# Hybrid attention and retention trunk on one core: a TensorE order written out at build time for the attention stage, the first query and key projection moved ahead of the last retention block, and part of the output projection run as filler

## The chip, the cores and the metric

The kernel runs on one core of one Trainium2 chip. The core has TensorE (PE in the profile, its weight loads apart as PEld), VectorE (DVE), ScalarE (ACT), GpSimd (POOL) and SyncE (SP), which issues most of the DMAs. The metric is the device time of one execution in microseconds, median of several runs.

## The reference, cut to what matters

Two layers, each the same; 1024 tokens, width 1024, everything in float32:

```python
def hybrid_layer(x, ...):
    proj = x @ w_in                      # fox q|k|v|forget logits, ret q|k|v|gate
    fox_out = fox_attention(q, k, v, log_sigmoid(f + b))   # 8 heads of 64, causal softmax,
                                         # logits = q k / 8 + c_i - c_j, c = cumsum(log_f)
    ret = groupnorm(retention_chunkwise(rotary(rq), rotary(rk), rv, gamma))   # 4 heads of 128
    mix = concat([fox_out, silu(rg) * ret]) @ w_out
    x = layernorm(ALPHA * x + mix)
    return layernorm(ALPHA * x + square(relu(x @ w_ff1)) @ w_ff2)
```

## The kernel before

Every float32 matrix is split into a rounded part and a rest (`split`, L159: ACT copies the rounded part, DVE subtracts), and a product is three PE matmuls (`mm3`, L229: low by high, high by low, high by high). One `mm3` over one slice of 128 inputs is thus three matmuls of 128x512; it is the unit called a step of filler below.

A layer runs in these stages (`layer`, L653). **Values and forget sums**: `project_values` (L309) and `forget_sums` (L338), which leaves the cumulated biases of all heads in the DRAM tensor c_d. **Retention**: for each of two pairs of heads, r = 0 and 1, `retention` (L370) projects queries and keys (block rqk), then gates and values (block rgv), eight token tiles each; the matmuls of scores and outputs follow two and three tiles later through `defer` and `tick`, and results go to r_d. **Queries and keys**: `project_qk` (L469) projects one pair p of attention heads in 36 steps (32 hold an `mm3`, four hold the evacuation) and writes q_d and k_d in DRAM; pair 0 comes right after the retention. **Attention** (`attention`, L495). **Output projection** in two column halves (L784 to L801). **Feed-forward**, a Strassen form in two parts (`feed_forward_in`, `feed_forward_out`).

Attention works on 32 blocks of steps (h, qq): head h, query rows 256*qq to 256*qq+255. For each it runs

- fronts (F; `front`, L525): for each of two row blocks one or two chunks of scores, two matmuls of queries by keys each (L541), and with the last chunk a mask matmul (L545). DVE adds the bias rel and takes the maximum (L547), ACT does the exponential (L553), DVE the reciprocal (L555), POOL scales (L556). A head has 12 chunks.
- backs (B; `back`, L560): for each pair of key blocks, a turn, 3 or 4 PE transposes of probabilities into one PSUM bank (L569), then a split into pt by ACT (L161) and DVE (L162). A head has 10 turns.
- values (V; `values`, L579): four matmuls per turn of pt by the values vp (L591); after every second block ACT and DVE add two halves (L604, L605), and for odd heads split them into mix.

`load` (L498) fetches queries, keys (ks) and values (vp) of a head from q_d, k_d and v_d, by SP, two buffers each. `load_bias` (L511) fetches one head's row of c_d to all partitions in ncb, one buffer, and `bias` (L518) makes rel from it on POOL, one buffer for each qq.

While attention runs, PE also gets filler, the generator `rest` (L699): `project_qk` of pairs 1 to 3 (108 steps), then `ret_transposes` (L488), eight groups of four PE transposes of retention outputs, each fetched from r_d into one buffer.

The program is written by a merge (L610): for block i the backs of i, the fronts of block i+2 (DEPTH = 2, L48) and a number of filler steps by `FILL` (L50): 18 for each head up to 5, then 4. Values trail the backs by up to 5 turns (LAG). That written order is only a priority: the scheduler of the framework places each instruction when its simulation finds it ready, PE's too, so later matmuls may fill earlier gaps. `load(h+1)` is called in block (h, 0) and `load_bias(h+1)` in block (h, 1), when fronts are at (h, 3); rel of (h, 3) is made by `bias` after the fronts of (h, 2). On SP, as on each engine, instructions then run in the order that the scheduler gave.

The output projection takes chunks of two 128-wide slices of the 1024 mixed inputs; slices 0 to 3 are the attention pairs, 4 to 7 retention. Its first half (L784 to L792) runs chunks in the order 4, 6, 0, 2 over eight token tiles in eight PSUM banks, its weights prepared up to two ahead (`weight`, L224, with a ring of four).

## Time and profile before

| | |
|---|---|
| median of 3 runs | 2405.14 us (2402.55 to 2405.2) |
| the profiled execution | 2406.83 us, of which the span 2404.8 us |
| PE busy | 2361.1 us, 98% of the span |
| DVE, ACT, POOL busy | 63%, 42%, 14% |
| mean granted PE clock | 0.997 of full speed |

Busy is the time in which at least one instruction of an engine is under way. Matmuls overlap: one of 128x512 lasts about 0.39 us, and one follows another in much less, so a short pause between two starts leaves PE busy. What a matmul costs is therefore read from the distance of starts. In the first layer attention runs from 313 to 517 us of the span, in the second from 1503 to 1707.

### The profile page before, as it was taken

The numbers are of one execution on the slowest core, as the hardware profiler recorded it, in microseconds if no ns is written. First come the engines' busy times: TensorE is split into PE (matmuls) and PEld (weight loads), VectorE is DVE, ScalarE is ACT, GpSimd is POOL, SyncE is SP. The second block draws the span as 40 slices with busy tenths as digits, with TensorE's granted clock in tenths as the row PEclk, the third lists the DMA queues.
The fourth block names the chain that finished last, engine by engine and source line by source line (L and its number), as shares of the span: only waits on it lengthen the run. The fifth ranks groups of instructions, "written<-read, shape, count | busy, mean of one in ns | idle before, by whom it ended". The sixth has DMA issues, their size and how long they took to land.

```text
span 2404.8 us, 32463 instructions
## 1 busy us (share of the span) xinstructions
PE 2361.1 (98%) x11888; PEld 1983.0 (82%) x11888; DVE 1510.0 (63%) x2703; ACT 1015.2 (42%) x1556; POOL 337.0 (14%) x469
## 2 busy tenths in 40 slices
PE   8999999999999999999999999999999999999997
PEld 8888887887888888888898888888888888888886
DVE  4655447854876667665755554588467766676557
ACT  3222246735544553434321212477274444543331
POOL 0223223500000000000202322244000000000003
PEclk9999999999999999999999999999999999999999
DMA  7465676433364458667555567664334544586664
GB/s 233 165 220 207 216 212 183 123 119 113 109 221 148 145 188 310 211 210 223 179 164 187 209 212 231 182 177 116 132 101 147 199 164 148 213 294 214 196 194 145
DMA packets 243807, 442.47 MB, mean 184 GB/s; under 512 B 26032, under 2 KB 128432, under 8 KB 235456
## 3 DMA queue, kind: packets, MB, share of 16 engines
q1 hardware_dynamic: 241344, 432.01, 55.2%
q10 hardware_dynamic: 2304, 8.39, 0.9%
q8 instruction: 94, 1.54, 0.3%
q14 instruction: 65, 0.53, 0.1%
HBM read 301.85 MB, written 138.48 MB: 183 GB/s over the span
## 4 chain that ended last, share of the span: by engine, by line
PE 88%; DMA 4%; DVE 4%; ACT 1%; issue 1%; SPq 0%; POOL 0%; DVEq 0%; ACTq 0%; POOLq 0%
PE mm L233 17%; PE qk L233 11%; PE qk L860 9%; PE tr L1070 7%; PE pv L1070 7%; PE pv L860 7%; PE qk L1070 5%; PE mm L1070 5%; PE mm L860 5%; PE tr L860 4%; PE tr L569 2%; PE qk L541 2%; PE pv L591 2%; DMA q_d<-ev 1%; PE pv L233 1%
## 5 line engine op out<-in xcount | busy, mean ns | idle before, releaser
L162 DVE TENSOR_TENSOR elo<-est,ehi 128x1024 fp32r<-128x1024 f32 x216 | 261.2, 1222 | 180.3 <-ACT ehi L161 179.4
L161 ACT CAST ehi<-est 128x1024 fp32r<-128x1024 f32 x216 | 226.7, 1054 | 343.4 <-PE pv L1070 127.5
L233 PE MATMUL mm<-whi,act 128*128 128x512 f32 (+1 forms) x608 | 187.9, 375 | 0.9 <-DVE act L162 0.5
L233 PE MATMUL qk<-whi,act 128*128 128x512 f32 (+1 forms) x608 | 186.6, 373 | 0.8 <-DVE act L162 0.8
L860 PE MATMUL qk<-xop,whi 128*128 128x512 f32 x608 | 187.3, 389 | 0.0
L161 ACT CAST whi<-wst 128x512 fp32r<-128x512 f32 (+1 forms) x140 | 115.9, 830 | 165.8 <-PE qk L233 36.0
L286 POOL TENSOR_SCALAR sd<-mv 128x1 f32<-128x1 f32 x15 | 13.9, 928 | 1211.4 <-DVE mv L283 1211.0
L860 PE MATMUL pv<-xop,whi 128*128 128x512 f32 x512 | 157.7, 389 | 0.0
L162 DVE TENSOR_TENSOR wlo<-wst,whi 128x512 fp32r<-128x512 f32 (+1 forms) x140 | 132.0, 946 | 39.2 <-ACT whi L161 38.6
L860 PEld LDWEIGHTS qk<-xop,whi 128*128 128x128 f32 x608 | 114.2, 188 | 23.6
L162 DVE TENSOR_TENSOR pt<-tr,pt 128x512 fp32r<-128x512 f32 (+1 forms) x160 | 99.7, 631 | 46.5 <-ACT pt L161 45.8
L233 PEld LDWEIGHTS mm<-whi,act 128*128 128x128 f32 x608 | 112.6, 192 | 19.7 <-ACT whi L161 0.8
L591 PE MATMUL pv<-pt,vp 128*128 128x256 f32 (+1 forms) x640 | 127.5, 302 | 0.2
L233 PE MATMUL mm<-act,whi 128*128 128x512 f32 x384 | 125.9, 396 | 0.0
L233 PEld LDWEIGHTS qk<-whi,act 128*128 128x128 f32 x608 | 110.3, 189 | 18.7 <-DVE act L162 1.0
L553 ACT ACTIVATE sc<-sc,mx 128x128 f32<-128x128 f32 (+7 forms) x128 | 99.4, 777 | 51.9 <-DVE mx L547 44.4
L860 PE MATMUL mm<-xop,whi 128*128 128x512 f32 x384 | 118.6, 390 | 1.5 <-DVE xop L162 1.5
L860 PE MATMUL qk<-xop,wlo 128*128 128x512 f32 x304 | 118.6, 390 | 0.0
L556 POOL TENSOR_SCALAR sc<-sc,ri 128x128 f32<-128x128 f32 (+7 forms) x128 | 96.8, 762 | 136.7 <-DVE ri L555 104.8
L161 ACT CAST pt<-tr 128x512 fp32r<-128x512 f32 (+1 forms) x160 | 85.8, 541 | 70.0 <-PE tr L569 67.9
L233 PE MATMUL mm<-wlo,act 128*128 128x512 f32 (+1 forms) x304 | 113.7, 374 | 0.7 <-DVE wlo L162 0.7
L860 PEld LDWEIGHTS pv<-xop,whi 128*128 128x128 f32 x512 | 96.1, 188 | 20.0
(278 smaller groups left out, 5942.8 us busy)
## 6 DMA issues: line engine op xcount, KB each, us to landing
est<-h_d SPq DMA_DIRECT2D x224, 256.0 KB, 3.6
wst<-in_w_ff_dram SPq DMA_DIRECT2D x76, 512.0 KB, 4.3
wr<-in_w_ff_dram SPq DMA_DIRECT2D x32, 1024.0 KB, 5.1
t_d<-ts SPq DMA_DIRECT2D x32, 1024.0 KB, 4.2
h_d<-hs SPq DMA_DIRECT2D x32, 1024.0 KB, 5.5
est<-t_d SPq DMA_DIRECT2D x128, 256.0 KB, 4.0
h_d<-rest SPq DMA_DIRECT2D x32, 768.0 KB, 5.7
est<-in_w_ff_dram SPq DMA_DIRECT2D x96, 256.0 KB, 4.8
```

The lines of the kernel that those rows point to most:

```text
L161: A.copy(hi, src)
L162: V.tensor_tensor(lo, src, hi.bitcast(F32), op=ALU.subtract)
L233: PE.matmul(ps, lhs(a, k), rhs(b, k), start=first and i == 0 and j == 0, stop=last and i == n - 1 and j == 2)
L286: G.tensor_scalar(sd, mv[:, :, 1], EPS, 1.0, op0=ALU.add, op1=ALU.mult)
L541: PE.matmul(ps[:, 0:w], qs[:, rb * P : rb * P + P], ks[part][:, c0 : c0 + w], start=part == 0, stop=part == 1 and not last)
L553: A.activation(sc[:, 0:ne], sc[:, 0:ne], AF.Exp, bias=mx, scale=-1.0, accum_out=sm)
L556: G.tensor_scalar(sc[:, 0:ne], sc[:, 0:ne], ri, 1.0, op0=ALU.mult, op1=ALU.mult)
L569: PE.transpose(tr[:, 2 * i + rb, :], probs[rb][:, j * P : j * P + P], ident)
L591: PE.matmul(ob[:, c + f * P : c + 256], vp[:, js[i], :], pt[b][:, 2 * i + f : 2 * i + 2, :], start=qq % 2 == 0 and jp == 0 and n == 0 and ...
L860: PE.matmul(ps, ops[p][a][:, k, :], right[p][b][:, k, :], start=first and k == 0 and n == 0, stop=last and k == 3 and n == 2, skip_group_c ...
L1070: PE.matmul(ps, ops[x_][:, 0, i * P : i * P + P], ops[y][:, 1, :], start=first and n == 0, stop=last and n == 2, skip_group_check=True)
```

## The change

A function `attention_order` writes the order of all attention work on PE as a list of letters: F one chunk, B one turn's transposes, V one turn's value matmuls, X one step of filler. It walks a model of DVE, ACT and POOL as three queues with durations written into it, and picks what is ready: V before B before F before X, but X first where filler is behind a goal, a line through fixed marks (30 steps before the first chunk, 36 by chunk 16, 72 by 40, 108 by 64, 128 by 96), with at most 4 steps ahead of it. Fronts may be 12 chunks ahead of the backs and three blocks of steps, and pt has three buffers. The letters alone reach the kernel; attention is emitted in their order in a region in which PE keeps the written order (where these instructions fall among PE's instructions from outside the region is left to the scheduler).

```diff
+DEPTH = 12
 QK_STEPS = 36
+WO_FIRST = 4
+RET_STEPS = 8
+WO_STEPS = 12
+SLACK = 4
+FIRST = 30
+LANDING = 9.0
+MARGIN = 1.2
+def attention_order():
...
+    qk_x = QK_STEPS * 3
+    last_x = qk_x + RET_STEPS + WO_STEPS
...
+        marks = ((0, FIRST), (16, 36), (40, 72), (64, 108), (len(chunks), last_x))
...
+        if nv < nb and nv in pt_ready:
+            found["V"] = pt_ready[nv] + MARGIN
...
+        if nb < len(turns) and nb - nv < PT_BUFS:
...
+                found["B"] = MARGIN + max(tr_free[nt % 2], *(prob[(i, rb)] for rb in (2 * qq, 2 * qq + 1)))
...
+            if nf - done < DEPTH and (i < 4 or nb >= len(turns) or turns[nb][0] > i - 4) and steps[i][0] in landed:
+                found["F"] = MARGIN / 2 + max(qk_free[nf % 2], landed[steps[i][0]])
+        if nx < last_x and nx < goal(nf) + SLACK:
...
+                found["X"] = max(tr_free[nt % 2] + MARGIN, rest_from[0])
...
+        if "X" in soon and nx < goal(nf):
+            pick = "X"
+        else:
+            pick = next((k for k in "VBFX" if k in soon), None)
...
+                rest_from[0] = t + 5.0
```

Pair 0 is projected between the blocks rqk and rgv of the last retention pair (its weights move in the load order with it), with a second evacuation buffer. For room, two tiles of the retention go from five buffers to four, and `forget_sums` reuses its small tiles.

```diff
+                if (name, r) == ("rgv", 1):
+                    for fox, c0 in (("fq", C_FQ), ("fk", C_FK)):
+                        spec((l, fox, 0), wi[:, :, c0 : c0 + 128])
...
+        between()
...
-            vt = pool.tile([P, 2, P], F32, tag="rvt", name=nm("rvt"), bufs=5)
+            vt = pool.tile([P, 2, P], F32, tag="rvt", name=nm("rvt"), bufs=4)
...
-                for r in range(2):
-                    retention(l, r, xT, part, cos, sin, gn, steps)
-                for _ in project_qk(l, 0, xT):
-                    pass
+                retention(l, 0, xT, part, cos, sin, gn, steps, lambda: None)
+                retention(l, 1, xT, part, cos, sin, gn, steps, lambda: [None for _ in project_qk(l, 0, xT, part)])
```

The filler gets 12 steps of the output projection: for token tiles 0 and 1, in the two banks of the tag mm, chunk 0 (4 steps) ahead of the retention transposes, chunks 4 and 6 (8 steps) behind them. The first half's chunks run as 0, 4, 6, 2. A retention row tile is fetched one group ahead, into two buffers.

```diff
         with tc.tile_pool(name=f"p2_{l}", bufs=1, reuse_waits="tile") as pool:
             def rest():
                 for p in range(1, FH // 2):
                     yield from project_qk(l, p, xT, pool)
-                yield from ret_transposes(mr, pool)
+                turning = ret_transposes(mr, pool)
+                for n, c in enumerate(order_c[:3]):
+                    wo_w[c] = weight(l, "wo", 0, c)
+                    for tt in range(2):
+                        if n == 0:
+                            wo_ps.append(ps_mm.tile([P, 512], F32, tag="mm", name=nm("mm")))
+                        for k in (c, c + 1):
+                            mm3(wo_ps[tt], lambda a, k: mixed(a, k, tt * P, P), lambda b, k: wo_w[c][b][:, k - c, :], (k,),
+                                k == order_c[0], False)
+                            yield
+                    if n == 0:
+                        yield from turning
...
+            with tc.manual_schedule(engines={mybir.EngineType.PE}):
+                attention(pool, mix, attention_order(), work)
```

In attention `load(h+1)` and, with it, rel of (h, 3) now come before the fronts of (h, 2); `load_bias(h+1)` and rel of (h+1, 0) before the fronts of (h, 3).

```diff
+        def all_fronts():
+            for i, st in enumerate(steps):
+                h, qq = st
+                if h + 1 < FH:
+                    if qq == 2:
+                        load(h + 1)
+                    if qq == 3:
+                        load_bias(h + 1)
+                if i + 1 < len(steps):
+                    bias(*steps[i + 1])
+                yield from front(h, qq, probs[st])
...
+        for what in order:
+            if what == "V":
+                values(*pvq.pop(0))
+            else:
+                next(kinds[what])
```

## Rows read from the trace of the kernel before

**Rows 1.** The profile page: busy time of each engine, share of the span, instructions.
```profile
PE 2361.1 (98%) x11888; PEld 1983.0 (82%) x11888; DVE 1510.0 (63%) x2703; ACT 1015.2 (42%) x1556; POOL 337.0 (14%) x469
```

**Rows 2.** Stretches: from:to us, length, busy us of each engine (instructions), PE clock, DMA share, GB/s.
```profile
277.00:313.00 36.00, 36.00 (x171) 30.17 (x170) 9.84 (x24) 8.21 (x14) 7.32 (x12) 1.00 0.85 258
313.00:398.00 85.00, 84.78 (x481) 70.81 (x479) 47.83 (x130) 41.73 (x86) 26.12 (x36) 1.00 0.57 169
398.00:449.00 51.00, 46.15 (x328) 38.66 (x326) 46.39 (x140) 40.29 (x89) 27.63 (x39) 0.97 0.66 182
449.00:517.00 68.00, 65.91 (x418) 55.80 (x417) 42.99 (x112) 37.42 (x79) 19.05 (x25) 1.00 0.31 89
1503.00:1588.00 85.00, 84.21 (x473) 70.21 (x472) 46.55 (x127) 40.23 (x84) 26.12 (x36) 1.00 0.60 174
1588.00:1638.00 50.00, 46.53 (x338) 38.77 (x337) 47.52 (x143) 41.78 (x92) 27.46 (x39) 1.00 0.67 186
1638.00:1707.00 69.00, 66.90 (x423) 56.51 (x422) 43.10 (x112) 37.33 (x78) 19.14 (x25) 1.00 0.31 88
```

**Rows 3.** Timeline of PE in a projection: start us, us, engine, line, instruction, count.
```profile
299.76 0.61 PE L233 MATMUL mm<-act,whi 128*128 128x512 f32 x2
300.21 0.39 PE L233 MATMUL mm<-act,wlo 128*128 128x512 f32 x1
300.44 0.61 PE L233 MATMUL mm<-act,whi 128*128 128x512 f32 x2
```

**Rows 4.** Timeline of PE in attention, two fronts back to back.
```profile
402.38 0.50 PE L541 MATMUL qk<-ks,qs 128*128 128x256 f32 x2
...
402.76 0.59 PE L541 MATMUL qk<-ks,qs 128*128 128x384 f32 x2
...
403.26 0.50 PE L569 MATMUL tr<-cst,sc 128*128 128x128 f32 x3
```

**Rows 5.** The second of those stretches for L233 alone: PE and PEld busy us (instructions).
```profile
313.00:398.00 85.00, 57.94 (x221) 38.90 (x219) 1.00 0.57 169
```

**Rows 6.** Groups on DVE, 313 to 398 us: count, busy us, mean ns, idle before.
```profile
L162 DVE TENSOR_TENSOR pt<-tr,pt 128x512 fp32r<-128x512 f32 (+1 forms) x21 | 13.1, 631 | 9.7 <-ACT pt L161 9.6
...
L547 DVE DVE_READ_ACCUMULATOR2_ANT mx<- 128x1 f32 x34 | 2.8, 83 | 0.0
```

**Rows 7.** Groups on DVE, 398 to 449 us.
```profile
L162 DVE TENSOR_TENSOR pt<-tr,pt 128x512 fp32r<-128x512 f32 (+1 forms) x30 | 18.5, 629 | 0.4 <-ACT pt L161 0.3
L547 DVE CUSTOM_DVE_ANT_0 sc<-qk,rel 128x512 f32<-128x512 f32 (+5 forms) x25 | 13.8, 552 | 3.0 <-PE qk L545 2.8 <-PE tr L569 0.2
L547 DVE CUSTOM_DVE_ANT_0 sc<-qk,rel,mx 128x512 f32<-128x512 f32 (+3 forms) x13 | 8.1, 621 | 0.3 <-PE qk L545 0.2
L605 DVE TENSOR_TENSOR ot<-ot,pv 64x512 f32<-64x512 f32 x6 | 4.1, 679 | 0.1
L555 DVE RECIPROCAL ri<-sm 128x1 f32<-128x1 f32 x25 | 3.7, 154 | 0.7 <-ACT sc L553 0.3 <-POOL rel L522 0.3
L162 DVE TENSOR_TENSOR mix<-ot,mix 128x512 fp32r<-128x512 f32 x3 | 3.4, 1122 | 0.0
L547 DVE DVE_READ_ACCUMULATOR2_ANT mx<- 128x1 f32 x37 | 3.0, 81 | 0.0
L162 DVE TENSOR_TENSOR wlo<-wst,whi 128x1024 fp32r<-128x1024 f32 x1 | 1.2, 1223 | 0.0
```

**Rows 8.** The chain that ended last, 400 to 425 us: start us, us, what.
```profile
404.25 10.80 DMA ncb<-c_d
...
415.88 0.70 POOL rel L522
...
419.17 0.55 PE tr L569 x3
```

**Rows 9.** All engines, the 5 us before that chain reaches PE again.
```profile
415.00:420.00 5.00, 3.13 (x26) 2.72 (x25) 3.36 (x13) 2.98 (x6) 4.77 (x7) 1.00 0.89 257
```

**Rows 10.** Waits of the SP queue, 280 to 520 us: total us, times, longest.
```profile
SPq L508 <- PE pv L591: 15.5, 1, 15.5
```

More of the change, by code (lines that the diff above doesn't have):

```diff
@@ L368, in forget_sums, with retention @@
         defer(2, finish)
-    def retention(l, r, xT, pool, cos, sin, gn, steps):
+    def retention(l, r, xT, pool, cos, sin, gn, steps, between):
         def project(name):
@@ L488, in ret_transposes, with fetch, go, attention @@
     def ret_transposes(mr, pool):
-        for tt in range(NT):
-            t = pool.tile([P, RH * RD], F32, tag="ev2", name=nm("rl"), bufs=1)
-            SP.dma_start(t, r_d[tt * P : tt * P + P, :])
-            transpose_in(mr, t, tt, groups=1)
-            yield
-    def attention(pool, mixes, fill, need, take):
+        rows_of = {}
+        def fetch(tt):
+            if tt % 2:
+                t = wp.tile([P, RH * RD], F32, tag="ev", name=nm("rl"), bufs=1)
+            else:
+                t = pool.tile([P, RH * RD], F32, tag="ev2", name=nm("rl"), bufs=1)
+            SP.dma_start(t, r_d[tt * P : tt * P + P, :])
+            rows_of[tt] = t
+        fetch(0)
+        def go():
+            for tt in range(NT):
+                if tt + 1 < NT:
+                    fetch(tt + 1)
+                transpose_in(mr, rows_of.pop(tt), tt, groups=1)
+                yield
+        return go()
+    def attention(pool, mixes, order, work):
         pv, heads, sums, rels, pvq, outs = {}, {}, {}, {}, [], {}
         def load(h):
-            qs = pool.tile([P, S], F32R, tag="qs", name=nm("qs"), bufs=2)
+            e = h % 2
+            qs = pool.tile([P, S], F32R, tag=f"qs{e}", name=nm("qs"))
             SP.dma_start(qs.bitcast(F32), q_d[h].rearrange("s d n -> (s d) n").bitcast(F32))
@@ L502, in load @@
             for part in range(2):
-                kt = pool.tile([P, S], F32R, tag=f"ks{part}", name=nm("ks"), bufs=2)
+                kt = pool.tile([P, S], F32R, tag=f"ks{part}{e}", name=nm("ks"))
                 for a in range(2):
@@ L506, in load @@
                 ks.append(kt)
-            vp = pool.tile([P, NT, P], F32R, tag="vp", name=nm("vp"), bufs=2)
+            vp = pool.tile([P, NT, P], F32R, tag=f"vp{e}", name=nm("vp"))
             SP.dma_start(vp.bitcast(F32), v_d[:, h].rearrange("(t p) s d -> p t (s d)", p=P).bitcast(F32))
@@ L609, in attention @@
         steps = [(h, qq) for h in range(FH) for qq in range(4)]
-        def merge(gens):
-            counts = [n for n, _ in gens]
-            done = [0] * len(gens)
-            live = [n > 0 for n in counts]
-            while any(live):
-                i = min((i for i in range(len(gens)) if live[i]), key=lambda i: (done[i] + 0.5) / counts[i] * (SPAN if i == 1 else 1.0))
-                done[i] += 1
-                if next(gens[i][1], gens) is gens:
-                    live[i] = False
@@ new lines, in all_fronts, with all_backs @@
+        def all_fronts():
[9 more added lines that the diff above has]
+                yield from front(h, qq, probs[st])
+        def all_backs():
+            for h, qq in steps:
+                yield from back(h, qq, probs[(h, qq)])
@@ L650, in attention @@
+        load_bias(0)
+        load(0)
+        bias(*steps[0])
+        kinds = {"F": all_fronts(), "B": all_backs(), "X": work}
+        for what in order:
+            if what == "V":
+                values(*pvq.pop(0))
+            else:
+                next(kinds[what])
         while pvq:
@@ L697, in layer, with mixed @@
         mr = Tokens(act, "act")
+        order_c, wo_w, wo_ps = (0, 4, 6, 2), {}, []
+        def mixed(part, c, t0, n):
+            if c < 4:
+                return mix[c][:, part, t0 : t0 + n]
+            return mr.at(part, c - 4, t0, n)
         with tc.tile_pool(name=f"p2_{l}", bufs=1, reuse_waits="tile") as pool:
@@ L701, in rest @@
                     yield from project_qk(l, p, xT, pool)
[L702 to L723 removed]
+                turning = ret_transposes(mr, pool)
[7 more added lines that the diff above has]
+                                k == order_c[0], False)
+                            yield
+                    if n == 0:
+                        yield from turning
+            work = rest()
+            with tc.manual_schedule(engines={mybir.EngineType.PE}):
+                attention(pool, mix, attention_order(), work)
             for _ in work:
                 pass
[L727 to L730 removed]
         right = {}
@@ L782, in norm @@
                         defer(2, first_half)
-                ps = banks(1) + banks(0)
-                order_c = (4, 6, 0, 2)
+                ps = wo_ps + [q.tile([P, 512], F32, tag=t, name=nm(t)) for q, t in ((ps_qk, "qk"), (ps_tr, "tr"), (ps_pv, "pv"))
+                              for _ in range(2)]
                 for c in order_c:
-                    w = weight(l, "wo", 0, c)
+                    w = wo_w.get(c) or weight(l, "wo", 0, c)
                     for tt in range(NT):
-                        mm3(ps[tt], lambda a, k: mixed(a, k, tt * P, P), lambda b, k: w[b][:, k - c, :], (c, c + 1),
-                            c == order_c[0], c == order_c[-1])
+                        if tt > 1 or c not in wo_w:
+                            mm3(ps[tt], lambda a, k: mixed(a, k, tt * P, P), lambda b, k: w[b][:, k - c, :], (c, c + 1),
+                                c == order_c[0], c == order_c[-1])
                         if c == order_c[-1]:
```

200 lines of the change are left out of this document (143 added, 57 removed).

## The prediction

> **What bounds the kernel now.** The page comes first: PE is busy 98% of the span, no other engine over 63% [rows 1]. The reader could stop there and think that nothing is left, but a matmul of 128x512 lasts 0.39 us and the next one starts 0.227 us after it (three starts in 0.68 us, from 299.76 to 300.44) [rows 3], so busy time hides short waits. The second view is the table of stretches [rows 2]. Idle PE is length less busy: nothing in 277 to 313; in the first layer's attention 0.22, 4.85 and 2.09 us, in the second's 0.79, 3.47 and 2.10, together 13.5 us. This is the lower bound of what PE loses to waits in attention.
>
> The middle stretch of each layer is the odd one: it holds no filler (the L233 matmuls, 221 in the first stretch [rows 5], end with it), DVE is busy 46.39 of 51 us and 47.52 of 50, and PE loses most there. For the loss by distance of starts I price attention work from the first stretch, where PE is idle for only 0.22 of 85 us. Its filler is 221 x 0.227 = 50.2 us, so 34.8 us went to 34 chunks of fronts (one maximum read each) and 21 turns (one pt each) [rows 6]. A chunk costs 0.38 and 0.50 us in two clean examples (402.38 to 402.76 to 403.26) [rows 4], I take 0.44; 15.0 us for the chunks leaves 19.8, or **0.94 us a turn** (transposes and values). At these prices the 37 chunks and 30 turns of 398 to 449 us [rows 7] are 16.3 + 28.2 = 44.5 us of PE work, and they took 51: 6.5 us lost, 1.34 times the idle time there. The factor over all six stretches gives 13.5 x 1.34 = **18.1 us** that waits cost both attentions. That is the most that a better order can give.
>
> One hole can be followed by name. The chain shows the bias row of the next head, issued at 404.25, landing 10.80 us later, then POOL's rel to 416.58, and PE's transposes at 419.17 [rows 8]; PE is busy 3.13 of the 5 us before that [rows 9]. From issue to rel it takes 12.3 us. Before, it is asked for while fronts are at (h, 3), four chunks ahead of the next head; at 51/37 = 1.38 us a chunk these are 5.5 us.
>
> **The change part by part.** PE's amount of work stays; what can change is the waits.
>
> Pair 0's projection moves: 32 steps of 0.68 us, 21.8 us of PE, trade places with the last retention block. PE had no idle time where it stood (36.00 of 36) [rows 2], so this gains nothing at once; it costs nothing either, as its eight writes to q_d and k_d now pass the last block's r_d writes on SP, and nothing reads those before the late transposes. The buffers that go from five to four are wanted again four tiles later and free after three, a tile being 24 matmuls or 5.4 us; if that cover went, one ACT copy would be late. The forget tiles' reuse: nothing, long before c_d is read. The last scores and outputs of the retention must mix with the first 30 filler steps; the region allows it, so 0. If they did not mix, some four dependent steps of DVE or ACT at 0.63 [rows 7] would show, 2.5 us a layer; nothing excludes up to that, and no gain.
>
> The order itself I price in three parts of attention per layer, PE work against DVE work. DVE's cost comes from the dense stretch: 46.39 less the weight split of 1.2 is 45.2 us, which its rows (28.6 us for fronts, 26.0 for turns, overlapping) share out as 0.64 us a chunk and 0.72 a turn [rows 7]. Where DVE was the fullest, the stretch took 51/46.39 = 1.10 and 50/47.52 = 1.05 times DVE's busy time [rows 2]; these are my two ends for a stretch that DVE bounds.
>
> - Chunks 0 to 16, thin in filler (six steps by the goal, four of slack, nine of them matmuls): PE 16 x 0.44 + about 8 turns x 0.94 + 9 x 0.68 = 20.7 us; DVE 10.2 + 5.8 + one evacuation 0.6 + two weight splits 2.4 = 19.0, times 1.05 to 1.10 is 20.0 to 20.9. Loss 0.
> - Chunks 16 to 64, 72 steps: PE 21.1 + 40 x 0.94 + 64 x 0.68 = 102 us; DVE 30.7 + 28.8 + 5.0 + 4.9 = 69. DVE's share, 68%, is nearer to the first stretch (56%, 0.22 idle) than to the dense ones: 0.5.
> - Chunks 64 to 96 and the turns behind them, up to 12 chunks late, some 37: PE 14.1 + 34.8 + twelve output projection steps 8.2 + eight groups of retention transposes at 0.4, under half a turn, 3.2 = 60.3 us; DVE 20.5 + 26.6 + eight splits 5.0 + three weight splits 3.7 = 55.8, so 58.6 to 61.4: loss 0 to 1.1, I take 0.6.
>
> Here stands a wait that had other work around it: each retention group needs its row tile, now fetched one group ahead. All of attention queues behind it on PE, but the groups stand 5 us apart in the plan and the row is asked for a group early; 0, and if it came late, the next transposes and with them DVE would idle.
>
> The bias row is now asked for before the fronts of (h, 3), and the last use of the old one, rel of (h, 3), comes before those of (h, 2): up to eight chunks of lead. That is 8 x 60.3/32 = 15.1 us late, 17 in the middle, and 10.3 at the start, against 12.3: two short once a layer. Backs can cover some of it, so 0 to 2.0, I take 1.0.
>
> A layer then still loses 0 + 0.5 + 0.6 + 1.0 = 2.1 us, both 4.2. **Gain 18.1 - 4.2 = 13.9 us**: 2406.8 - 13.9 = 2392.9 for an execution like the profiled one, which lies 1.7 above the median of its runs; 2391.2 on the median's scale.
>
> **Weighed against a rule.** Weight loads keep PEld busy 83% of the stretch with filler (70.81 of 85 us) and 76% of the one without (38.66 of 51) [rows 2]. The Trainium skill (Perfetto Trace Analysis, Identifying the Most-Contended Engine) says to judge TensorE's headroom by the busy share of weight loads and not by that of matmuls. By it the loss before would be 11.0 us and not 18.1, and the gain 6.8 and not 13.9 (third rival). The trace agrees that the busy share of matmuls hides waits; against the other half speaks the mix, since the dense stretch has no 512-wide matmul of L233 and 8.4 loads per us of PEld where the first has 6.8.
>
> **The rivals.**
>
> *All waits go.* The order leaves 18.1 us and nothing new: 2387. For it: DVE fits on average in every part. Against: the first and last part leave it under 5% to spare.
>
> *Less was lost than I think.* The turn's price may be wrong where nothing but fronts and turns runs. Taking PEld's 83% in the first stretch as full, the busy times of the five others stand for 46.4, 67.0, 84.3, 46.5 and 67.8 us, so that 4.6, 1.0, 0.7, 3.5 and 1.2 were lost, 11.0 in all [rows 2]; 11.0 - 4.2 = 6.8 remain: 2398.3. Against it: this is under the 13.5 us in which PE had no matmul at all.
>
> *Waits move.* The thin first and last parts, 81 us a layer, lose the share of the dense stretch, 6.5/51: 10.3 us a layer, 20.6 in all against 18.1 now: 2407, no change. For it: DVE is as full there as PE. Against: fronts may run 12 chunks ahead, where they had two blocks.
>
> *Slower: loads behind a blocked one.* Values now trail fronts by up to 12 chunks, and `load(h+1)` waits for the last values of h-1 before its vp; one such wait lasted 15.5 us already [rows 10]. If the bias row queues behind it on SP, the fronts of the next head find no rel, and PE, whose order is fixed, stands. There are 14 changes of head; it decides from (18.1 - 4.2)/14 = 1.0 us each. At 1.7 us each they cost 23.8: 2415. Against: the wait must exceed some 3 us beyond the lead.
>
> **How the numbers follow.** Chances: forecast 0.40, all waits go 0.20, less lost 0.10, waits move 0.15, slower 0.15. About 0.2%, 4.8 us, is what can be told from no change, so faster means below 2400.3: nearly all of the forecast, the second, and some of the third, 0.66. Same: the waits that move and the edges of the rest, 0.19. Slower: 0.15. The range goes from 2383 (all waits, and 4 us for prices set too low) to 2409, which takes in the moved waits and leaves most of the slower case out.
>
> **What would show it.** Right: attention without a filler-free stretch, so that L233 appears throughout; PE idle per layer under 2 us where it was 6 to 7; no PE wait behind ncb; DVE over 90% busy only in the last part. Wrong: transposes or fronts waiting for rel or ncb at changes of head, PE idle behind the retention's last outputs, or DVE idle in the first and last parts while PE waits too.

## The result and the profile after

The changed kernel takes **2423.14 us** (median of four runs, 2420.57 to 2425.7) against 2405.17 for the kernel before, measured beside it on the same chip: ratio 1.0075, 95% interval 1.0057 to 1.0092. It is slower by 18 us where 14 us of gain were forecast. The profiled execution has a span of 2420.4 us at a mean granted clock of 0.993, 15.6 us more than before.

The page's first line, against [rows 1], tells nothing: PE is still "98%" busy, and with the same number of instructions.

```profile
PE 2365.1 (98%) x11888; PEld 1991.5 (82%) x11888; DVE 1502.8 (62%) x2703; ACT 1017.4 (42%) x1556; POOL 335.8 (14%) x469
```

The stretches of attention, as in [rows 2] (from:to us, length, busy us of PE, PEld, DVE, ACT, POOL with instructions, PE clock, DMA share, GB/s), cut where the loss begins and ends:

```profile
280.00:314.00 34.00, 34.00 (x178) 29.11 (x177) 15.95 (x45) 10.37 (x21) 10.24 (x19) 1.00 0.71 227
314.00:326.00 12.00, 7.29 (x30) 5.30 (x29) 2.58 (x11) 2.75 (x7) 4.39 (x7) 0.86 1.06 302
326.00:440.00 114.00, 113.24 (x718) 97.12 (x717) 83.05 (x235) 75.19 (x157) 47.86 (x68) 1.00 0.61 179
440.00:484.00 44.00, 36.26 (x233) 30.73 (x232) 32.66 (x96) 28.39 (x63) 18.34 (x24) 0.88 0.65 184
484.00:526.00 42.00, 41.58 (x245) 35.79 (x244) 17.57 (x41) 14.87 (x28) 4.56 (x5) 1.00 0.04 14
1503.00:1518.00 15.00, 11.33 (x51) 8.99 (x50) 2.79 (x5) 4.22 (x6) 4.76 (x7) 1.00 0.97 255
1518.00:1629.00 111.00, 110.17 (x682) 93.82 (x681) 78.98 (x228) 70.30 (x148) 45.13 (x64) 0.99 0.66 192
1629.00:1675.00 46.00, 39.33 (x255) 33.47 (x254) 33.96 (x96) 30.55 (x65) 19.73 (x27) 0.93 0.60 167
1675.00:1716.00 41.00, 40.03 (x241) 34.11 (x240) 21.06 (x54) 18.20 (x38) 7.38 (x9) 1.00 0.13 46
```

The reader is to see two things. The middle became what it was meant to be: 114 us with 0.76 us of idle PE in the first layer and 111 us with 0.83 in the second, where before the dense 51 us of the first layer alone lost 4.85. The loss sits in two short stretches, the start (4.71 us idle of 12, first layer) and 440 to 484 us (7.74 of 44), and both run in part at a lower clock. DVE is busy only 32.66 of those 44 us, 74%.

The waits of PE over the whole run name what it lacks (engine, line waited for: us in total, times, longest):

```profile
PE qk L742 <- DMA ks<-k_d: 8.4, 4, 3.0
PE tr L439 <- DMA rl<-r_d: 6.5, 2, 3.5
...
PE tr L439 <- DVE pt L340: 5.5, 6, 1.3
```

Neither DMA wait is among the waits of before. L742 is the fronts' score matmul, L439 the helper that transposes, here a retention row: two late loads a layer, head 0's keys and the first retention row.

**The start.** PE's timeline (start, us, engine, line, instruction, count, idle before it):

```profile
314.40 0.61 PE L414 MATMUL mm<-act,whi 128*128 128x512 f32 x2
317.99 0.36 PE L742 MATMUL qk<-ks,qs 128*128 128x256 f32 x1 [2.97 <-DMA ks<-k_d]
320.08 0.58 PE L742 MATMUL qk<-ks,qs 128*128 128x256 f32 x1 [1.74 <-DMA ks<-k_d]
```

and SP's queue ahead of it:

```profile
305.51 3.31 SPq L640 DMA_DIRECT2D r_d<-on  x2
308.86 0.42 SPq L714 DMA_DIRECT2D ncb<-c_d  x1
309.38 0.41 SPq L701 DMA_DIRECT2D qs<-q_d  x1
309.88 2.49 SPq L706 DMA_DIRECT2D ks<-k_d  x4
```

By the program, head 0's loads go into memory that the retention holds to its end; the trace shows them on SP right behind its last r_d writes. In the kernel before, the last r_d write left at 292.29 and the keys at 304.92:

```profile
292.29 0.33 SPq L455 DMA_DIRECT2D r_d<-on  x1
304.92 5.11 SPq L505 DMA_DIRECT2D ks<-k_d  x8
```

Now the last r_d write leaves 16 us later (SP ends it at 308.8), since pair 0's projection precedes the last block, and the keys 5 us later. The 30 steps of filler end at 315.0, and the first two score matmuls, which wait for the keys, start at 318 and 320. In the kernel before, the DMA engines were just as full in that place, but pair 0's matmuls covered the loading (PE 14.00 of 14 us at a DMA share of 1.06):

```profile
300.00:314.00 14.00, 14.00 (x64) 11.62 (x63) 2.61 (x3) 3.42 (x4) 3.34 (x5) 1.00 1.06 303
```

**The late part.** SP's queue again, then PE's timeline:

```profile
438.31 1.24 SPq L668 DMA_DIRECT2D k_d<-ev  x2
...
441.46 2.39 SPq L706 DMA_DIRECT2D ks<-k_d  x4
443.95 0.54 SPq L681 DMA_DIRECT2D rl<-r_d  x1
```

```profile
446.04 0.72 PE L789 MATMUL pv<-pt,vp 128*128 128x256 f32 x4
446.60 0.49 PE L770 MATMUL tr<-cst,sc 128*128 128x128 f32 x3
446.84 0.71 PE L742 MATMUL qk<-ks,qs 128*128 128x512 f32 x2
451.04 1.08 PE L439 MATMUL tr<-cst,rl 128*128 128x128 f32 x4 [3.48 <-DMA rl<-r_d]
...
453.72 1.09 PE L789 MATMUL pv<-pt,vp 128*128 128x256 f32 x4
454.62 1.08 PE L770 MATMUL tr<-cst,sc 128*128 128x128 f32 x4
```

The row for token tile 0 goes into ev2, the buffer from which pair 3's last k_d write is still leaving. It is asked for when that write has landed, behind four key loads, and lands 7.0 us after its issue, where the median row takes 2.6. PE, whose order is fixed, stands 3.48 us before it. The filler is spread to the end of the middle here: pair 3's last filler matmul starts at 436.5, and the row is there 14.5 us after it. The model behind the order allows 9.0 (LANDING in the diff).

**The clock.** At the long waits the granted clock goes from 1.00 to 0.50, that is from 2.4 to 1.2 GHz; the row of a stretch cut to the lower level shows it:

```profile
449.50:456.30 6.80, 5.26 (x24) 4.68 (x25) 1.96 (x5) 2.59 (x5) 1.83 (x2) 0.50 0.45 121
```

There are five such stretches inside the two attentions (3.4, 6.8, 3.4, 3.4 and 6.8 us, 23.8 together, PE busy for 21.6 of them) against one of 3.4 us before. Four of them lie at the waits for keys and rows; the fifth, from 463.1, follows two waits of 0.49 and 1.25 us. In the rows above four value matmuls take 0.56 us at the higher level (446.04 to 446.60) and 0.90 at the lower (453.72 to 454.62), a speed of 0.62: by these rows the lower clock costs 21.6 x 0.38 = 8.2 us, an estimate, where it cost 1.3 before. It is a low one: two filler matmuls that start at 321.12, at the lower level, take 0.86 us to the next start, 0.43 each against 0.227.

Idle PE in attention, as the prediction summed it, is now 25.8 us against 13.5. The 12.3 more and the clock's 6.9 more make 19.2 us, against 15.6 between the spans; that the surplus is short waits, hidden in PE's busy time, which the fixed order now avoids in the middle is argued, not shown.

**What came as predicted.** The filler runs nearly throughout; L414 alone, the line of the filler (L233 in [rows 5]), in three stretches:

```profile
326.00:440.00 114.00, 55.31 (x201) 35.29 (x199) 1.00 0.61 179
440.00:484.00 44.00, 2.87 (x11) 1.56 (x9) 0.88 0.65 184
484.00:526.00 42.00, 26.74 (x105) 18.86 (x105) 1.00 0.04 14
```

The last line holds the output projection's own matmuls too. POOL's waits for the bias row (ref behind ncb) fell from 83.6 to 34.1 us, and PE waits for no rel at a change of head.

### The profile page after: what moved, and what is told of

It is laid out like the page before. It is cut to its first block, busy times and chain, and to the rows that moved or that the text cites. A ratio compares the mean times of both kernels' runs of the same rounds, so it can differ in the third digit from the quotient of the medians.

```text
span 2420.4 us, 32442 instructions
## 1 busy us (share of the span) xinstructions
PE 2365.1 (98%) x11888; PEld 1991.5 (82%) x11888; DVE 1502.8 (62%) x2703; ACT 1017.4 (42%) x1556; POOL 335.8 (14%) x469
## 5 line engine op out<-in xcount | busy, mean ns | idle before, releaser
L414 PE MATMUL mm<-whi,act 128*128 128x512 f32 (+1 forms) x544 | 166.7, 372 | 1.0 <-DVE act L340 0.5
L414 PE MATMUL qk<-whi,act 128*128 128x512 f32 (+1 forms) x544 | 164.8, 370 | 0.8 <-DVE act L340 0.8
L414 PE MATMUL mm<-act,whi 128*128 128x512 f32 x512 | 160.5, 394 | 0.0
L742 PE MATMUL qk<-ks,qs 128*128 128x512 f32 (+4 forms) x384 | 112.0, 386 | 8.9 <-DMA ks<-k_d 8.4
L414 PEld LDWEIGHTS mm<-whi,act 128*128 128x128 f32 x544 | 99.9, 192 | 17.1 <-ACT whi L339 0.9
L414 PEld LDWEIGHTS qk<-whi,act 128*128 128x128 f32 x544 | 98.4, 189 | 16.7 <-DVE act L340 1.0
L414 PEld LDWEIGHTS mm<-act,whi 128*128 128x128 f32 x512 | 96.9, 190 | 17.6
```

Of the source, the lines that this page charges most:

```text
L414: PE.matmul(ps, lhs(a, k), rhs(b, k), start=first and i == 0 and j == 0, stop=last and i == n - 1 and j == 2)
L742: PE.matmul(ps[:, 0:w], qs[:, rb * P : rb * P + P], ks[part][:, c0 : c0 + w], start=part == 0, stop=part == 1 and not last)
```

## The experiments

Each ran three rounds (the last two five) beside the kernel before, whose median was 2405.0, 2404.2, 2405.4, 2405.0 and 2405.7 us in the five batches. "Ratio" is against it, with the 95% interval. An interval reaches 0.0009 to 0.0016 either way, 2 to 4 us, so a step of 2 or 3 us between two runs is not by itself told from noise. "Less DVE work" (e13 to e15) leaves out the rests of the transposed probabilities, 80 subtractions a layer; the rounded part stands in for them, so PE's matmuls stay the same and the result is less exact.

| run | what | us | ratio |
|---|---|---|---|
| e1_swap | changed kernel, first retention row in the other buffer | 2414.0 | 1.0040 [1.0024, 1.0056] |
| e2_nomove | changed kernel, pair 0 back behind the retention | 2419.5 | 1.0061 [1.0045, 1.0077] |
| e3_swap_nomove | both | 2410.1 | 1.0023 [1.0013, 1.0033] |
| e4_move | kernel before, pair 0 moved | 2418.6 | 1.0057 [1.0042, 1.0073] |
| e16_move_ev2 | the same with the change's buffers | 2418.8 | 1.0058 [1.0043, 1.0073] |
| e9_after_free | changed kernel, no fixed order | 2408.6 | 1.0014 [1.0005, 1.0023] |
| e6_free | e3, no fixed order | 2405.7 | 1.0003 [0.9993, 1.0012] |
| e5_ret_late | e3, retention rows behind the last front | 2407.4 | 1.0015 [1.0006, 1.0025] |
| e8_first | e3, 38 steps ahead of the first front | 2407.0 | 1.0012 [1.0003, 1.0021] |
| e7_bias | e3, bias row asked for earlier | 2409.5 | 1.0018 [1.0009, 1.0028] |
| e12_late38 | e5 and e8 together | 2405.4 | 1.0001 [0.9991, 1.0010] |
| e10_mid_fixed | e5, fixed from front 12 to 64 only | 2409.5 | 1.0018 [1.0008, 1.0028] |
| e11_start_free | e5, fixed from front 12 on | 2405.2 | 1.0002 [0.9992, 1.0011] |
| e13_before_dve | kernel before, less DVE work | 2388.7 | 0.9934 [0.9919, 0.9949] |
| e14_late38_dve | e12, less DVE work | 2394.6 | 0.9962 [0.9949, 0.9976] |
| e15_after_dve | changed kernel, less DVE work | 2412.0 | 1.0029 [1.0017, 1.0041] |
| e17_before_pool | kernel before, some subtractions on POOL | 2408.2 | 1.0010 [1.0001, 1.0019] |
| e18_late38_pool | e12, the same | 2407.0 | 1.0006 [0.9997, 1.0015] |

### Two late loads, each undone alone and both

```diff
 # e1: the even rows take the buffer that is free early
-            if tt % 2:
+            if tt % 2 == 0:
                 t = wp.tile([P, RH * RD], F32, tag="ev", name=nm("rl"), bufs=1)
 # e2: pair 0 behind the retention again (its weights in the load order too)
-                retention(l, 1, ..., lambda: [None for _ in project_qk(l, 0, xT, part)])
+                retention(l, 1, ..., lambda: None)
+                for _ in project_qk(l, 0, xT, part):
+                    pass
```

> The changed kernel with one edit: retention row tiles of even number go into the buffer ev and odd ones into ev2, so that the first row no longer waits for the last k_d write out of ev2. Theory (the first retention group stalls PE 3.5 and 3.2 us on a row that is fetched late, and PE then runs 6.8 us at half clock in each layer): the wait on rl in the first group goes, and with it most of the half-clock stretch behind it; 4 to 6 us a layer, 8 to 12 us less than the changed kernel, so about 2412. Rival (the late part is bound by DVE, the row only shows it first): the stall moves to the next wait and the time stays within 2 us of 2423.

> The changed kernel with pair 0's projection back behind the last retention block; order list, filler and buffers stay. Theory (the move takes away the 21.8 us of PE work that covered the loads of head 0, which start only when the retention's tiles are free; PE stalls 4.7 us on ks and runs 3.4 us at half clock): the wait of the first fronts on ks goes, 5 to 7 us a layer, 10 to 14 us less than the changed kernel, about 2411. Rival (the loads of head 0 are late for another reason, the written order puts 30 filler steps before the first front however long the loads take): the first front still waits for ks and the time stays within 3 us of 2423.

> Both edits of the two runs before at once. If the two stalls are separate places of loss, the gains add: 18 to 26 us less than the changed kernel, 2397 to 2405, at or under the kernel before. If they share something (the clock, the DMA queue), the sum is clearly less than both gains: above 2408.

Against 2423.1 the swap gives 9.1 us, as expected, and the move back 3.6, where 10 to 14 were expected. Both give 13.0, short of the 18 to 26 expected: the two gains as measured add. In e1 the wait for rl falls from 6.5 to 0.9 us, and those for ks stay (10.2, four times). In e2 the waits for ks go and that for rl stays (6.2). So each wait belongs to its own edit. But the move's 3.6 us is a net: with pair 0 back, another wait of the fixed order takes the place of head 0's keys (4.9 us for POOL in e3, 5.2 in e2). This is e3, PE and POOL in turn:

```profile
324.37 0.66 PE L767 MATMUL tr<-cst,sc 128*128 128x128 f32 x3 [2.43 <-POOL sc L754]
```

```profile
323.46 0.20 POOL L713 TENSOR_SCALAR ref<-ncb 128x4 f32<-128x4 f32 x1 [4.47 <-DMA ncb<-c_d]
323.63 0.69 POOL L754 TENSOR_SCALAR sc<-sc,ri 128x512 f32<-128x512 f32 x1
```

POOL's queue holds ref of head 1, which waits for its bias row, ahead of the scaling that the first transposes need. And in e3 a third late load comes to light, which the wait for the row had covered: the keys of head 6, the first of pair 3, which can be read only behind pair 3's last k_d write; 3.4 us over both layers.

```profile
449.10 0.35 PE L739 MATMUL qk<-ks,qs 128*128 128x256 f32 x1 [2.07 <-DMA ks<-k_d]
```

### The move of pair 0 alone

```diff
 # e4: on the kernel before
-                for r in range(2):
-                    retention(l, r, xT, part, cos, sin, gn, steps)
-                for _ in project_qk(l, 0, xT):
-                    pass
+                retention(l, 0, ..., lambda: None)
+                retention(l, 1, ..., lambda: [None for _ in project_qk(l, 0, xT)])
 # e16: also project_qk(l, 0, xT, part), the two tiles of four buffers and the forget tiles' reuse
```

> The kernel before with only pair 0's projection moved ahead of the last retention block; order by the scheduler as before. Theory (the move by itself makes the loads of head 0 late): the first front starts later against the work done, but filler is not limited to 30 steps here, so PE stays busy: 0 to 4 us slower than before, 2405 to 2409, with the middle stretch still empty of filler. Rival (the move is harmless or a gain and only the fixed order makes it a loss): within 1 us of 2405 or faster.

> The kernel before with pair 0 moved ahead of the last retention block, now with the second evacuation buffer for it, four in place of five of the two retention tiles and the reuse of the forget tiles, as the change has it. Alone, without that buffer, the move cost 13.6 us. Theory (that cost was the one buffer, whose write stood on SP behind head 0's loads): most of it goes, 2406 to 2410, no wait for ev, 3 to 5 us left for keys that land later. Rival (the late keys and the retention's last outputs beside the filler cost the 13.6 themselves): 2414 to 2419.

e4 lies outside both of its ranges; in e16 the rival holds. They agree: the move costs 13.6 and 13.8 us in the old order, and pair 0's second evacuation buffer has no part in that. The wait that shows most is pair 1's, the same in both (e4; 10.6 us in two waits in either kernel):

```profile
332.42 0.79 PE L236 MATMUL mm<-act,wlo 128*128 128x512 f32 x1 [5.56 <-DVE ev L162]
```

PE waits for the evacuation, which needs the buffer of a q_d write. SP issued that write only behind the loads of two heads, and it took 11.2 us to land, where the median of the q_d and k_d writes from 300 to 336 us is 3.9:

```profile
308.69 0.42 SPq L504 DMA_DIRECT2D qs<-q_d  x1
309.20 2.42 SPq L509 DMA_DIRECT2D ks<-k_d  x4
...
313.39 3.34 SPq L509 DMA_DIRECT2D ks<-k_d  x4
317.44 0.38 SPq L512 DMA_DIRECT2D vp<-v_d  x1
318.61 2.10 SPq L487 DMA_DIRECT2D q_d<-ev  x2
```

```profile
331.06 0.58 ACT L161 CAST ev<-mm 128x512 fp32r<-128x512 f32 x1 [5.48 <-DMA q_d<-ev]
```

PE's waits for POOL's scaling grow too (7.2 us against 2.1 before), and 17 us of attention run at the lower clock against 3.4. So attention's first loads, all leaving only after a later end of the retention, cost in either order; which instruction meets them differs. The Trainium skill (DMA: Bandwidth & Descriptors, Anatomy of one DMA) says that DMA engines wait on no semaphores, the issuing sequencer does, before it sends the transfer. The trace agrees that SP itself stands: in the first layer's attention of the changed kernel it stood 18.6 us in four waits for old values to be read before it could issue vp (L709), one of 10.2 us.

### Is it the late data or the fixed order?

```diff
 # e9 on the changed kernel, e6 on e3
-            with tc.manual_schedule(engines={mybir.EngineType.PE}):
-                attention(pool, mix, attention_order(), work)
+            attention(pool, mix, attention_order(), work)
```

> The kernel of both edits with attention emitted in the order of the list, but without the region that fixes it on PE; the scheduler may move matmuls. Theory (the list is kept by PE in the middle without waits, and the losses come from loads and banks that the scheduler's simulation does not see either): within 4 us of 2410. Rival (fixing the order is what hurts, the scheduler would fill the holes): at least 5 us faster, 2405 or less.

> The changed kernel without the region that fixes PE's order; the list of letters is only a priority then. Pair 0 stays ahead of the last retention block and the first retention row stays in the late buffer, so head 0's keys and that row land as late as in the changed kernel (7 and 9 us a layer between them). Theory (the fixed order turns late data into PE idle time, since nothing behind the waiting instruction may pass it): the scheduler puts filler or fronts into both holes, no wait for rl and little for ks, no half clock late, and the time falls by 10 us or more, to 2405 to 2413. Rival (late data cost as much in any order, because what stands behind depends on them too or the other work has run out): 2417 to 2423. The start could split: there 30 filler steps are done and only pair 1's steps remain, of which the order takes none before the first chunk, and a free order may take them.

With the same list as a mere priority, the time falls by 14.5 us in e9. The two stretches that lost 4.71 and 7.74 us lose 0.43 and 2.22, at full clock:

```profile
314.00:326.00 12.00, 11.57 (x55) 8.92 (x54) 2.65 (x8) 3.80 (x7) 2.83 (x4) 1.00 1.06 308
400.00:440.00 40.00, 37.19 (x263) 31.33 (x261) 35.97 (x112) 32.53 (x75) 23.24 (x32) 1.00 0.66 170
440.00:484.00 44.00, 41.78 (x282) 34.80 (x282) 34.89 (x101) 30.30 (x67) 19.39 (x27) 1.00 0.55 154
```

But only at the start is the datum as late as before: the keys leave SP at 309.23 (309.88 in the changed kernel), the first front starts at 317.40 (317.99), and filler fills the hole. Late, the row itself is in time. The scheduler drew the filler forward, so pair 3's last k_d write left at 391.51 and not at 438.31, and the row 52 us before it is used:

```profile
395.76 0.33 SPq L681 DMA_DIRECT2D rl<-r_d  x1
447.35 0.60 PE L439 MATMUL tr<-cst,rl 128*128 128x128 f32 x4
```

The price is the stretch without filler, which is back; L414 alone, 400 to 420 us (10.71 us in the changed kernel):

```profile
400.00:420.00 20.00, 0.00 (x0) 0.00 (x0) 1.00 0.67 182
```

PE is idle for 2.81 us from 400 to 440, where the fixed order loses less than 1 in the whole middle. So at the start the fixed order turns late keys into idle time; in the late part the even spread of filler, which was the aim, is what makes the row late, and the fixed order then waits for it. Where these two loads are in time (e3 to e6) the fixed order still costs 4.4 us; e6, just outside both of its ranges, has no filler from 400 to 420 either.

### What is left when the loads are in time

```diff
 # e5, on e3: in attention_order, a retention row is no candidate while fronts are left
+                if nf == len(chunks):
                     found["X"] = max(tr_free[nt % 2] + MARGIN, rest_from[0])
 # e8, on e3
-FIRST = 30
+FIRST = 38
-        marks = ((0, FIRST), (16, 36), ...
+        marks = ((0, FIRST), (16, 40), ...
 # e7, on e3: at fronts (h, 2)
-                        load(h + 1)
+                        bias(*steps[i + 1])
+                        load_bias(h + 1)
+                        load(h + 1)
```

> The kernel of both edits (row buffers swapped, pair 0 back) in which the order list puts the eight retention transposes only behind the last front; the late part of attention keeps 4 steps of filler. Theory (in the late part PE loses to the retention groups, which as third user of the two transpose banks wait for DVE's pt, and not to a lack of filler): idle PE in the 45 us of the late part falls from some 4.7 us to under 2.5, time 3 to 6 us lower, 2404 to 2407. Rival (the late part is short of filler, any would do): idle stays or grows, time 2409 to 2414.

> The kernel of both edits in which rel of (h, 3) and the bias row of the next head are asked for before the other loads of that head, at the fronts of (h, 2). Theory (at the first change of head POOL stands 4.5 us before ref, waiting for ncb, with the scaling of probabilities queued behind it; PE then waits 2.4 us on that scaling and runs 3.4 us at half clock): the wait of the transposes on POOL goes in the start part, 2 to 4 us a layer, 4 to 8 us in all, 2402 to 2406. Rival (the row is late because SP is held by other entries, the place in the program changes nothing): within 2 us of 2410.

> The kernel of both edits with 38 steps of filler ahead of the first front, not 30 (and 40 by chunk 16, not 36). Theory (the start loses to loads of heads 0 and 1 that come late against the filler ahead of them): the waits on ks and ncb in the start part shrink, 2 to 5 us less in all, 2405 to 2408. Rival (the loads are tied to the fronts and move with them): same losses, within 2 us of 2410, or slower, since the middle then has eight steps less.

> The wholly fixed kernel with pair 0 back, rows swapped, retention groups behind the last front (2407.4), and 38 steps of filler ahead of the first chunk in place of 30. Theory (two separate remainders, late and start, add): 2407.4 less the 3 us that 38 steps gave alone, 2403.5 to 2405.5. Rival (the eight steps moved forward are missed in the middle or late): 2407 to 2410.

Two small terms are told from noise only together (e3 to e12, 4.7 us). The retention rows were a third user of the two transpose banks: the waits of L439 for pt, 5.5 us in the list above, are gone in e5, and idle PE from 436 to 481 us falls from 6.74 to 3.59; 2.7 us. Eight more steps ahead of the first front give 3.1 alone and 2.0 on top of e5. e7 stays within its rival's 2 us, but not for the rival's reason: SP did issue the row earlier, at 311.23 and not at 316.37. But ref could start only 10.7 us after that and not 7.1, and, now ahead of all scalings in POOL's queue, it held the first three up as well:

```profile
321.89 0.20 POOL L713 TENSOR_SCALAR ref<-ncb 128x4 f32<-128x4 f32 x1 [11.70 <-DMA ncb<-c_d]
```

PE's wait for POOL fell only from 4.9 to 3.9 us. In e12 these terms are mended together, as its theory had it, and it is level with the kernel before. Its stretches in the first layer, cut alike:

```profile
310.00:332.00 22.00, 20.41 (x104) 16.13 (x103) 9.09 (x28) 8.98 (x19) 4.88 (x9) 1.00 0.89 288
332.00:436.00 104.00, 102.43 (x657) 87.98 (x656) 76.63 (x217) 68.47 (x145) 44.15 (x62) 1.00 0.59 165
436.00:481.00 45.00, 41.78 (x289) 35.34 (x288) 38.95 (x120) 33.71 (x73) 21.41 (x28) 1.00 0.49 124
481.00:526.00 45.00, 44.08 (x242) 37.21 (x241) 20.13 (x32) 13.77 (x24) 1.77 (x2) 1.00 0.38 130
```

Idle: 1.59, 1.57, 3.22 and 0.92 us, 7.3 in the layer and 7.4 in the other by the same cuts, 14.7 together against 13.5 before. No half clock is left, and of late loads only head 6's keys, 1.0 us in the first layer and 0.6 in the second: the waits have moved from the stretch without filler to the start, the middle and the last 45 us of fronts, where DVE is busy 87%.

### Free at the ends

```diff
 # on e5: only the letters from front 12 (e11), or from front 12 to 64 (e10), inside the region
+        emit(order[:a])
+        with tc.manual_schedule(engines={mybir.EngineType.PE}):
+            emit(order[a:b])
+        emit(order[b:])
```

> Pair 0 back behind the retention, the even rows in the buffer that is free early, retention groups only behind the last front (the kernel of 2407.4), and PE's order fixed only from front 12 to front 64; before and behind, the list is a priority. Theory (the fixed order gains where filler is plentiful, 5 to 6 us a layer in the stretch that held none, and loses 3 to 4 us a layer at the start and late where it can't fill holes): both gains come together, 2396 to 2400, faster than before by 0.2% to 0.4%. Rival (what the free order saves late it takes from work that the middle needs, or the total is set by DVE in the late part): 2403 to 2408, no difference from before.

> As the kernel that is fixed from front 12 to front 64, but fixed from front 12 to the end. Theory (start and late part each carry some of the loss of the fixed order): the start gives 2 to 3 us a layer, 2401 to 2404, between the wholly fixed kernel (2407.4) and the one that is free late as well (2396 to 2400). Rival (only the start costs): equal to the kernel that is free late as well, within 1.5 us.

e11 gives 2.2 us against e5, short of what was expected. e10 misses: with the late part free as well it loses 4.3 us instead of gaining. Its stretch from 436 to 481 us has 41.18 us of busy PE against 41.96 in e11 and a granted clock of 0.96 against 1.00. PE waits there for head 6's keys, 3.7 us over both layers against 1.5; the rest of the 4.3 us stays open.

### How much of it is DVE

```diff
 # e13 on the kernel before, e14 on e12, e15 on the changed kernel
-                split(pt[0][:, f:4, :], pt[1][:, f:4, :], tr[:, f:4, :])
+                A.copy(pt[0][:, f:4, :], tr[:, f:4, :])
 ...
+                pt = [pool.tile([P, 4, P], F32R, tag="pt0", ...)] * 2
```

> The kernel before without DVE's part of the split of the transposed probabilities: the rounded part stands in for the rest as well, so PE's matmuls stay in number and shape and DVE loses 80 subtractions of 0.63 us a layer. Theory (the waits of before are waits for DVE, worth the 18.1 us of the prediction's sum): the time falls by 14 to 20 us, to 2385 to 2391. Rival (part of that sum is no wait but what each group of matmuls behind a semaphore takes, which no order gives back; DVE's waits are worth half of it or less): 2395 to 2400.

> The same left out of the wholly fixed kernel with 38 steps ahead and the late repairs (2405.4). Theory (its losses are as large as before's and only stand elsewhere, at the start and in the last part, where DVE is as full as PE): it falls by as much as before does, within 4 us. Rival (its remainder is the fixed order itself, whatever DVE does): it falls by less than half as much as before does.

> The same left out of the changed kernel. Theory (its 18 us over before are late data, head 0's keys and the first retention row, and half-clock stretches behind them, not DVE): it stays 12 to 20 us above the kernel before with the same left out. Rival (DVE's work is what makes the late row and keys cost): it comes within 6 us of it.

The kernel before falls by 16.3 us: PE's work is the same, so all of it was waiting. The total of 11.0 us of the rival "less was lost", two thirds of that, was thus too low. The Trainium skill (Perfetto Trace Analysis, Identifying the Most-Contended Engine) names the busy share of weight loads, beside the share of peak arithmetic, for judging TensorE's headroom; to take the 83% of the first stretch as full, which gave the 11.0, was the prediction's own step. e12 falls by 10.8, between the two expectations: two thirds of before's fall, so most of what it still loses goes with DVE, and it stays 5.9 us above e13. Its stretch from 436 to 481 us with less DVE work:

```profile
436.00:481.00 45.00, 43.34 (x304) 37.46 (x303) 25.43 (x88) 33.96 (x74) 21.28 (x27) 1.00 0.44 117
```

1.66 us idle where it was 3.22. The changed kernel stays 23.4 us above the kernel before with the same left out, more than was expected even of the theory: its loss is no DVE matter.

```diff
 # e17 on the kernel before, e18 on e12: the rests of mix, and of the weights of pairs 1 to 3
-                    split(m[:, 0, hs], m[:, 1, hs], ot)
+                    A.copy(m[:, 0, hs], ot)
+                    G.tensor_tensor(m[:, 1, hs], ot, m[:, 0, hs].bitcast(F32), op=ALU.subtract)
```

> The kernel before with two kinds of subtraction moved from DVE to POOL, with nothing left out: the rest of the mixed outputs (8 a layer at 1.1 us) and the rests of the query and key weights of pairs 1 to 3 (6 a layer at 1.2 us), some 16 of the 50 us that leaving out the splits of the probabilities took from DVE. Theory (DVE's work is what the remaining waits stand on, 16.3 us for 50 us a layer): about a third of it, 3 to 6 us, 2399 to 2402. Rival (POOL then scales the probabilities later, and the transposes wait for it instead): 2404 to 2410.

> The same move in the wholly fixed kernel with 38 steps ahead and the late repairs (2405.4), whose last part DVE fills to 86%. Theory: 2 to 5 us, since a part of the moved work lies in the middle, where DVE is not the bound: 2400.5 to 2403.5. Rival (POOL's longer subtraction delays the scaling, and a fixed order waits for it): 2405 to 2412.

Relieving DVE without leaving work out did not come off: 2408.2 and 2407.0. On POOL a weight's subtraction takes 2.5 us where DVE took 1.2 [rows 7]. In both the rival holds. In e17's profile the dense stretch is nearly full (50.27 of 51 us) and PE waits elsewhere, 3.5 us for mix from POOL and 3.0 for evacuations; that execution took 2403.7 us, 4.5 less than the median of its runs, so what the others lost is not in it. Of all runs with the whole computation none beats the kernel before; four versions are level with it (e6, e11, e12, e18), the best 18 us faster than the change.

## Why the prediction was wrong, step by step

- **The total of 18.1 us of waits** is borne out: 16.3 us came back in e13 as soon as DVE had less to do, with 1.97 us still idle in its dense 51. What fell is the belief that an order alone gets them.
- **The middle**, 0.5 us a layer: right (0.76 idle of 114 and 0.83 of 111; 0.7 to 0.9 of 104 in e3 and e5).
- **"It costs nothing either" (pair 0's move)** is the first step that failed. It looked at PE, where pair 0 stood without idle time, at SP's writes passed and at the buffers, and not at what pair 0's 21.8 us were cover for: attention's first loads, into memory that the retention frees. Price: 13.6 us in the old order, 3.6 net in the new.
- **"0" for the wait of the retention rows** is the second, and the larger in the change: 9.1 us. The text saw that the row is asked for a group early; for the first row there is no group before it, and its buffer is the one that pair 3's evacuation uses last, late because the filler is now spread. The row came 14.5 us after pair 3's last filler matmul and not 9. That all of attention queues behind the wait was said there, and is what happened.
- **The start, 0, and the late part, 0.6**: e3 has 2.61, 6.74 and 0.00 us idle at the start, late and behind in the first layer. Of the late loss, 2.7 us in both layers are the transpose banks (e5) and 3.4 in e3 head 6's keys, which the text did not have; most of the rest goes with DVE (e14), which in e12 is busy for 87% of that stretch and not at the 92% (55.8 of 60.3) that the sum took to cost next to nothing. With 3.22 and 2.98 us lost at that load in the two layers, averages over 45 us say too little about which engine waits when.
- **The bias row**, 1.0: no PE wait for rel at a change of head; where it came too late in the runs (e3), it was head 1's, and PE met it through POOL's queue, which the sum did not look at.
- **The retention's tail**, 0: right, 34.00 of 34 us from 280 to 314.
- **The clock** had no term. By the estimate above the stretches at 1.2 GHz cost 6.9 us more than before, about half as much again as the 12.3 us of added idle time.
- **The rivals.** "Waits move", 2407 at 0.15, is what the kernel does when its late loads and the place of the retention rows are mended (2405.4 to 2407.4): the loss of the filler-free stretch turns up mainly at the thin start and end. "Loads behind a blocked one", 2415, had the right queue and the wrong place: not 14 changes of head, but two loads a layer where memory changes hands between stages.

The account from 2391.2 to 2423.1, by medians: 13.0 us for the two late loads (e3), 2.7 for the transpose banks (e5) and 2.0 for the start (e12), these two sure only as a sum, and 14.2 that stay in e12, of which leaving out DVE work returns 10.8.

## What to carry to other kernels

A TensorE order fixed at build time turns a datum that is later than the model says into idle time of the whole engine: head 0's keys, equally late in both, cost 4.71 us of the first layer in the fixed order and 0.43 in the free one. And whoever spreads filler also moves its last write, and with it every load that waits for that write or its buffer. So before fixing an order, list for each load the last user of its buffer, and what stands ahead of it on its queue, above all at the borders of stages; or fix only stretches that have no load of their own. And when a step without idle time is moved away, ask what it was hiding where it stood.

## What was not expected of the hardware

The size of what follows a short wait: PE had been busy to 447.6 us and stood 3.48 us; the granted clock fell to 0.50 at 449.5, while PE stood, and rose again at 456.3, so that the first 5.3 us of work ran at the lower level, where a group of four matmuls took 0.90 instead of 0.56 us. In e3 a wait of 2.43 us was followed by 3.4 us at the lower level too. In e9, e6 and e12 no stretch of attention's profile shows the lower level, and there PE's longest waits are 0.6, 0.7 and 1.7 us.
